# PE in the source's order through the attention, and score rows written bank by bank

## The chip, the cores and the metric

The kernel runs on one core of a Trainium2 chip. The metric is device microseconds of one execution. TensorE (PE) does the matmuls, VectorE (DVE), ScalarE (ACT) and GpSimd (POOL) the rest, and SyncE (SP) issues the DMAs. Each engine works through its own list of instructions in a fixed order and waits on semaphores for the others.

## The reference

Two layers of a block with three branches that read one normalised input: a Mamba-2 scan, grouped-query attention (four heads of 64) and differential attention (four heads, each with two softmax maps that share their values). The width is 1024, and there are 256 context tokens ahead of 1024 latent ones. This case is about the two attention branches:

```python
def block(qblk):
    s = jnp.einsum('bqgrd,bsgd->bgrqs', qblk, k).astype(jnp.float32) * scale
    p = jax.nn.softmax(s, axis=-1).astype(v.dtype)
    return jnp.einsum('bgrqs,bsgd->bqgrd', p, v)
...
o = attention(q[:, :, 0::2], k[:, :, 0::2], v) - lam * attention(q[:, :, 1::2], k[:, :, 1::2], v)
...
o_l = jnp.concatenate([y_s_l, y_g_l, y_d_l], axis=-1) @ w_out[l]
```

Context tokens read context alone, latent tokens read both (1280 keys). The second layer gives no context output.

## The kernel before

**Jobs.** Each layer has a projection and scan stage, then an attention stage, then a tail. The attention stage (from line 1226) works through jobs. A job is one head of one kind (0: grouped-query, keys in tile `gk`; 1: differential, keys in `dk`) for two or four tiles of 128 queries, and `CORD` orders the jobs of the last four query tiles: gk, dk, dk, gk, dk, dk, gk, gk. A job is taken in halves of two query tiles. A full half has five **steps**, one for each two of the ten key tiles; layer 0 has 168 steps and layer 1 has 160.

**Scores.** `s_rows` (line 1228) scores a pair of rows of 128 x 1280. A pair is two query tiles of a gk head, or the two maps of one query tile of a dk head. It takes five PSUM banks `sc` of a pool of three (`NSC`): two of 512 for the first row, one that holds the last 256 of both rows, two of 512 for the second. PE writes them (line 1239; two matmuls for a bank of 512 in a gk head, one in a dk head, so 12 and 6 for a pair), DVE copies each bank to `pt` and keeps its minimum (line 1241), reduces the minima (1252), and ACT takes the exponential with a row sum (1254). For a dk pair DVE then makes a factor `cc` (1284, 1285) and subtracts the second map from the first in 1024 columns (1289); POOL does the other 256 (1293, 1294).

**A step.** `w_front` transposes four 128 x 128 blocks of `pt` on PE (1369) into one of two PSUM tiles `tp`; ACT copies that to `pf` (1379), DVE or ACT rounds it to `ph` (1391, 1389), and POOL computes the remainder `pl` (the helper on line 128). `w_back` multiplies `ph` and `pl` with the values (1411, 1412) for the step two before (`LAG` is 3). After a job `out_b` folds the result (`pr`, 1335) and `y_out` transposes it (1309). Each step also takes its share of `fills`: the output projection (`ops`, lines 342 to 344) and, in layer 0, the modulation of the next layer (`mps`, line 149), whose weights `wm` come in pairs of 512 KB into the three buffers of tag `wo`.

**The source's order.** The loop at the end of `block_kernel` writes a step as `w_front`, then scores if any are owed, then `w_back`, then `out_b`/`y_out` that are due, then fills. Scores are owed when the share of the score work done is under the share of the value work done plus a lead of 30 (`LEAD`, in units of a quarter step), and while fewer than eight of the ten `pt` buffers are taken. Ahead of the first step of a half, every pair that the half needs and that isn't written yet is written at once. `s_next` (1449) writes a whole pair.

**The program's order.** The tile scheduler takes these instructions with priorities from the source's order (`w_front` and `w_back` are put 50 places ahead) and places them, engine by engine, by readiness in a timeline of its own. So PE's list isn't the source's: a score or a transpose can stand ahead of value matmuls that were written earlier.

**Loads.** When the last pair of a job is written, `prefetch` loads the next head of its kind: `dk` (1049, 1280 KB) and `q` (1050), or `q` alone or with `gk` (1043, 1042). `dk`, `gk` and each kind's `q` have one buffer, so these loads wait for the last score matmul that reads the old head.

Of the kernel before, what the change touches and what calls it, by code (L numbers as in the profile page):

```python
# [14 lines left out]
PSUM = bass.MemoryType.PSUM  # L15
# [28 lines left out]
CORD = ((0, 0), (1, 0), (1, 1), (0, 1), (1, 2), (1, 3), (0, 2), (0, 3))  # L44
TRIG = 12, 6
ILV = 0
SPC = 0
CSEQ = ((0, 0), (0, 1), (1, 0), (1, 1), (2, 0), (2, 1), (3, 0), (3, 1), (4, 0), (4, 1), (5, 0), (5, 1), (6, 0), (6, 1), (7, 0), (7, 1))
SCR = 1.3
MP = 1, 2  # L50
# [11 lines left out]
NSC, NTP, NPO, NXO = 3, 2, 1, 2  # L62
# [5 lines left out]
def block_kernel(ctx: ExitStack, tc: tile.TileContext, tok, cvec, wmod, pack,  # L68
# [4 lines left out]
    def pool(name, bufs=1, **kw):  # L73
        return tc.tile_pool(name=name, bufs=bufs, reuse_waits="tile", **kw)
# [354 lines left out]
    for l in range(DEPTH):  # L429
# [794 lines left out]
        wlast = [o7.tile([P, 8, P], F32R, name=f"wlast{i}") for i in range(2)]  # L1224

        with pool("att", 2) as ap, pool("attX", NXO, space=PSUM) as aX, pool("attO", NPO, space=PSUM) as aO, \
                pool("attS", NSC, space=PSUM) as aS, pool("attT", NTP, space=PSUM) as aT_:
            def s_rows(jb, pair):

                full = jb.nk == NT  # L1230
# [218 lines left out]
            def s_next():  # L1449
# [3 lines left out]
                with shifted(HPS):  # L1453
                    while s_at:
                        if next(s_at[0], 1):
                            s_at.pop()
                        if SPC:
                            break
# [163 lines left out]
```

## Time and profile before

| | us |
|---|---|
| time, median of 3 runs | 2074.26 (2069.14 to 2074.6) |
| the profiled execution | 2063.46 |
| its span, first to last instruction | 2061.6 |
| PE busy | 1806.6 (88%) |
| DVE busy | 1428.5 (69%) |
| POOL busy | 1211.7 (59%) |
| ACT busy | 1041.5 (51%) |

The profiled execution was 10.8 us shorter than the median. The attention stages are the stretches 604 to 1092 us and 1614 to 2025 us of the span. A busy PE in this profile is a union of overlapping matmuls with modelled ends, so a gap in it is surely idle, and a busy stretch need not be PE at its peak.

### The profile page before, as it was taken

To read this page: it belongs to the slowest core of one execution; us is meant where nothing else is said; L and a number is where in the kernel's file an instruction comes from. 1 tells how busy PE (TensorE), PEld (TensorE's weight loads), DVE (VectorE), ACT (ScalarE), POOL (GpSimd) and SP (SyncE) were. 2 spreads that over 40 slices of the span, in tenths; PEclk is the share of its full clock that TensorE was granted. 3 is DMA by queue.
4 is the path that set the end of the run, shared out by engine and by line. 5 is a ranking of instruction groups with operands and counts; after the bars stand their busy time and mean duration, and the time that the engine had idled before them with its cause. 6 is when DMAs were issued, how large, how long until landed. Compare 5 with 4: busy or idle time off the path is not lost. (4 is left out here: it accounts for less than half of the span.)

```text
span 2061.6 us, 30333 instructions
## 1 busy us (share of the span) xinstructions
PE 1806.6 (88%) x9936; PEld 1471.4 (71%) x9936; DVE 1428.5 (69%) x3286; ACT 1041.5 (51%) x1955; POOL 1211.7 (59%) x1135
## 2 busy tenths in 40 slices
PE   4899989899879999988988799888899899989895
PEld 3677777787668667876775487777777777878783
DVE  4777566766538776698866578468656588788954
ACT  3445233334437775766654345234244477777661
POOL 3626245747616676777755326466567378787761
PEclk9899999899999999998989899999999999999897
DMA  9157546776786788786656138667766866557545
GB/s 290 47 170 271 152 165 191 236 235 176 222 259 198 245 263 257 234 256 202 211 191 214 63 102 280 226 183 231 244 202 204 260 185 192 157 155 237 161 152 205
DMA packets 359998, 418.57 MB, mean 203 GB/s; under 512 B 38753, under 2 KB 252833, under 8 KB 359841
## 3 DMA queue, kind: packets, MB, share of 16 engines
q1 hardware_dynamic: 359840, 416.64, 65.1%
q8 instruction: 78, 1.28, 0.3%
q14 instruction: 80, 0.65, 0.1%
HBM read 282.18 MB, written 134.38 MB: 202 GB/s over the span
## 5 line engine op out<-in xcount | busy, mean ns | idle before, releaser
L128 POOL TENSOR_TENSOR pl<-pf,ph 128x512 fp32r<-128x512 f32 x283 | 373.6, 1325 | 189.0 <-DVE ph L1391 69.7
L1241 DVE TENSOR_SCALAR_CACHE_REDUCE pt<-sc 128x512 f32<-128x512 f32 (+1 forms) x600 | 334.2, 587 | 78.5 <-PE sc L1239 63.4
L958 PE MATMUL prj<-wh,u 128*128 128x512 f32 (+1 forms) x768 | 296.6, 389 | 33.0 <-DVE th L964 18.1
L1254 ACT ACTIVATE pt<-pt,nm 128x1280 f32<-128x1280 f32 x192 | 262.3, 1366 | 92.1 <-DVE nm L1252 91.0
L959 PE MATMUL prj<-wl,u 128*128 128x512 f32 (+1 forms) x768 | 294.8, 384 | 10.3 <-POOL wl L128 7.8
L960 PE MATMUL prj<-wh,u 128*128 128x512 f32 (+1 forms) x768 | 291.7, 380 | 0.0
L1369 PE MATMUL tp<-ident,pt 128*128 128x128 f32 x1312 | 209.3, 285 | 14.0 <-ACT pt L1254 5.6
L1379 ACT COPY pf<-tp 128x512 f32<-128x512 f32 x289 | 166.8, 581 | 74.9 <-PE tp L1369 49.3
L1412 PE MATMUL po<-pl,vt 128*128 128x256 f32 x644 | 183.1, 307 | 15.6 <-POOL pl L128 14.7
L958 PEld LDWEIGHTS prj<-wh,u 128*128 128x128 f32 x768 | 151.8, 199 | 62.5 <-DVE th L964 19.9
L1411 PE MATMUL po<-ph,vt 128*128 128x256 f32 x644 | 186.0, 303 | 5.2 <-DVE ph L1391 2.9
L1369 PEld LDWEIGHTS tp<-ident,pt 128*128 128x128 f32 x1312 | 162.1, 147 | 37.9 <-ACT pf L1379 10.7
L959 PEld LDWEIGHTS prj<-wl,u 128*128 128x128 f32 x768 | 152.0, 198 | 38.0 <-POOL wl L128 11.2
L960 PEld LDWEIGHTS prj<-wh,u 128*128 128x128 f32 x768 | 151.7, 198 | 23.5
L1239 PE MATMUL sc<-dk,q 128*128 128x512 f32 (+1 forms) x400 | 146.1, 408 | 15.2 <-DVE pt L1241 12.0
L1412 PEld LDWEIGHTS po<-pl,vt 128*128 128x128 f32 x644 | 126.3, 196 | 33.0 <-POOL pl L128 25.3
L1411 PEld LDWEIGHTS po<-ph,vt 128*128 128x128 f32 x644 | 127.2, 197 | 19.4 <-DVE ph L1391 5.6
L606 DVE SCALAR_TENSOR_TENSOR cacc<-craw,hw,cacc 128x1284 f32<-128x1284 f32 (+1 forms) x64 | 120.0, 1877 | 28.0 <-ACT cacc L603 12.0
L581 PE MATMUL prj<-u,wTh 128*128 128x512 f32 x256 | 109.8, 429 | 22.2 <-DVE u L209 14.2
L1239 PE MATMUL sc<-gk,q 128*128 128x256 f32 (+1 forms) x400 | 110.0, 385 | 19.9 <-DVE pt L1241 16.7
L342 PE MATMUL ops<-y,wo 128*128 128x512 f32 (+1 forms) x304 | 117.7, 387 | 10.5 <-DMA y<-y 6.3
L582 PE MATMUL prj<-u,wTh 128*128 128x512 f32 x256 | 109.3, 427 | 7.4 <-DVE u L128 6.8
(277 smaller groups left out, 4310.7 us busy)
## 6 DMA issues: line engine op xcount, KB each, us to landing
wo<-wo SPq DMA_DIRECT2D x80, 512.0 KB, 4.9
wm<-in_wmod_dram SPq DMA_DIRECT2D x48, 512.0 KB, 6.2
dk<-dk SPq DMA_DIRECT2D x16, 1280.0 KB, 7.9
ab<-acs SPq DMA_DIRECT2D x18, 1024.0 KB, 7.5
wo<-wos SPq DMA_DIRECT2D x32, 512.0 KB, 3.7
wf<-in_wtok_dram SPq DMA_DIRECT2D x64, 256.0 KB, 4.4
y<-y SPq DMA_DIRECT2D x30, 512.0 KB, 5.7
op<-o SPq DMA_DIRECT2D x48, 256.0 KB, 4.4
```

The lines of the kernel that those rows point to most:

```text
L128: eng.tensor_tensor(out_, full, hi.bitcast(F32), op=ALU.subtract)
L606: V.scalar_tensor_tensor(acc[:, a0:1284], raw[:, a0 + j:1284 + j], hw[:, i * 5 + j:i * 5 + j + 1], acc[:, a0:1284], op0=ALU.mult, op1=ALU.add)
L958: TE.matmul(ps[:, c0:], uh, wh[k][:, c0:], start=k == 0, stop=False)
L959: TE.matmul(ps[:, c0:], uh, wl[k][:, c0:], start=False, stop=False)
L960: TE.matmul(ps[:, c0:], ul, wh[k][:, c0:], start=False, stop=k == KT - 1)
L1239: TE.matmul(ps[:, 0:b - a].rearrange("p (t c) -> p t c", c=P), q[:, jb.q0 + j], kt[:, a // P:b // P], start=x == 0, stop=x == len(qq) - 1)
L1241: V.tensor_scalar(ts[r][:, a:b], ps[:, 0:b - a], -1.0, None, op0=ALU.mult, op1=ALU.min, accum_out=mts[r][:, i:i + 1])
L1254: S_.activation(e, e, AF.Exp, bias=nm, scale=-1.0, accum_out=jb.s2[:, j, mp_:mp_ + 1])
L1369: TE.transpose(tp[:, j * P:(j + 1) * P], jb.pt[2 * hf + j % 2][:, cs(2 * s + j // 2)], ident)
L1379: S_.copy(pf[:, :w_], tp[:, :w_])
L1411: TE.matmul(o, vv, a[:, c], start=k == 0, stop=False)
L1412: TE.matmul(o, vv, b[:, c], start=False, stop=k == jb.nk - 1)
```

## The change

`SPC` goes from 0 to 1: `s_next` leaves its loop after one piece of a pair, so an owed score is one bank (one of the five pieces; a sixth call does the dk combination). The rule by which scores are owed is the same, and it is asked again before each piece. And the attention stage runs under a manual schedule for PE: PE's instructions of this stage keep the order in which the source writes them. DVE, ACT, POOL and SP are still placed by the scheduler.

```diff
--- before.py
+++ after.py
@@ -44,7 +44,7 @@
 CORD = ((0, 0), (1, 0), (1, 1), (0, 1), (1, 2), (1, 3), (0, 2), (0, 3))
 TRIG = 12, 6
 ILV = 0
-SPC = 0
+SPC = 1
 CSEQ = ((0, 0), (0, 1), (1, 0), (1, 1), (2, 0), (2, 1), (3, 0), (3, 1), (4, 0), (4, 1), (5, 0), (5, 1), (6, 0), (6, 1), (7, 0), (7, 1))
 SCR = 1.3
 MP = 1, 2
@@ -1224,7 +1224,8 @@
         wlast = [o7.tile([P, 8, P], F32R, name=f"wlast{i}") for i in range(2)]
 
         with pool("att", 2) as ap, pool("attX", NXO, space=PSUM) as aX, pool("attO", NPO, space=PSUM) as aO, \
-                pool("attS", NSC, space=PSUM) as aS, pool("attT", NTP, space=PSUM) as aT_:
+                pool("attS", NSC, space=PSUM) as aS, pool("attT", NTP, space=PSUM) as aT_, \
+                tc.manual_schedule(engines={mybir.EngineType.PE}):
             def s_rows(jb, pair):
 
                 full = jb.nk == NT
```

Below, `tp` are the transposes of a step, `sc` the scores (from `dk` or `gk` keys), `po` the value matmuls, `ops` the projection, `mps` the modulation, `bps` a broadcast row. In the changed kernel lines past 1227 are one higher.

PE before, layer 1, while the scores of the last dk head's second half are written; other work stands between the banks:

```order
L1239 MATMUL sc<-dk,q 128x512
L1369 MATMUL tp<-ident,pt 128x128 x4
L1412 MATMUL po<-pl,vt 128x256
L1411 MATMUL po<-ph,vt 128x256
L1412 MATMUL po<-pl,vt 128x256
L1239 MATMUL sc<-dk,q 128x512
L1239 MATMUL sc<-dk,q 128x256
L1369 MATMUL tp<-ident,pt 128x128 x4
L1239 MATMUL sc<-gk,q 128x512 x2
L1409 MATMUL po<-pf,vt 128x256 x2
```

PE now, at the start of that head's second half:

```order
L194 MATMUL bps<-ident,nrr 128x128 x4
L1240 MATMUL sc<-dk,q 128x512 x2
L1240 MATMUL sc<-dk,q 128x256 x2
L1240 MATMUL sc<-dk,q 128x512 x4
L1240 MATMUL sc<-dk,q 128x256 x2
L1240 MATMUL sc<-dk,q 128x512 x2
L1370 MATMUL tp<-ident,pt 128x128 x4
L1412 MATMUL po<-ph,vt 128x256
L1413 MATMUL po<-pl,vt 128x256
```

All banks of both pairs of this half stand in one block, and the transposes that read these very rows come right behind it; nothing of another step is between.

PE before, layer 1, from the last rows ahead of the first score on a newly loaded dk head (`dk_19057`); the last score on the old one (`dk_18424`) stands 35 instructions above it:

```order
L1412 MATMUL po_16198<-pl_18771,vt_17999 128x256
L1411 MATMUL po_16198<-ph_18790,vt_17999 128x256
L1335 MATMUL pr_18851<-fold_78,ot_18674 128x64 x2
L1412 MATMUL po_16198<-pl_18791,vt_17999 128x256
L1411 MATMUL po_16198<-ph_18790,vt_17999 128x256
L1412 MATMUL po_16198<-pl_18791,vt_17999 128x256
L1369 MATMUL tp_18890<-ident_67,pt_18507 128x128
L1369 MATMUL tp_18890<-ident_67,pt_18508 128x128
L1369 MATMUL tp_18890<-ident_67,pt_18507 128x128
L1369 MATMUL tp_18890<-ident_67,pt_18508 128x128
L1411 MATMUL po_16198<-ph_18843,vt_17999 128x256
L1239 MATMUL sc_19137<-dk_19057,q_19056 128x512
```

PE now, the same change of heads (`dk_18509` to `dk_19135`):

```order
L1240 MATMUL sc_19106<-dk_18509,q_18508 128x512
L1412 MATMUL po_16205<-ph_19048,vt_18068 128x256
L1413 MATMUL po_16205<-pl_19049,vt_18068 128x256
L1412 MATMUL po_16205<-ph_19048,vt_18068 128x256
L1413 MATMUL po_16205<-pl_19049,vt_18068 128x256
L1370 MATMUL tp_19121<-ident_67,pt_18694 128x128
L1370 MATMUL tp_19121<-ident_67,pt_18801 128x128
L1370 MATMUL tp_19121<-ident_67,pt_18694 128x128
L1370 MATMUL tp_19121<-ident_67,pt_18801 128x128
L1240 MATMUL sc_19144<-dk_19135,q_19134 128x512
```

Between the last score on the old head and the first on the new one eight matmuls are left, one step's value matmuls and the next one's transposes. In layer 0 the same place has 21 in between (70 before).

PE before, layer 0, in the modulation of the next layer:

```order
L149 MATMUL mps<-wm,s_82 32x512 x2
L1239 MATMUL sc<-gk,q 128x512 x2
L1239 MATMUL sc<-gk,q 128x256 x2
L1239 MATMUL sc<-dk,q 128x256
L149 MATMUL mps<-wm,s_82 32x512 x2
L1411 MATMUL po<-ph,vt 128x256
L1335 MATMUL pr<-fold,ot 128x64 x2
L1239 MATMUL sc<-dk,q 128x256
L149 MATMUL mps<-wm,s_82 32x512 x2
L1412 MATMUL po<-pl,vt 128x256
```

PE now, there:

```order
L149 MATMUL mps<-wm,s_82 32x512 x4
L1370 MATMUL tp<-ident,pt 128x128 x4
L1240 MATMUL sc<-dk,q 128x512 x2
L1412 MATMUL po<-ph,vt 128x256
L1413 MATMUL po<-pl,vt 128x256
L1412 MATMUL po<-ph,vt 128x256
L1413 MATMUL po<-pl,vt 128x256
L149 MATMUL mps<-wm,s_82 32x512 x4
L1370 MATMUL tp<-ident,pt 128x128 x4
```

The two weights of one k stand together, once in a step, in 16 of 19 steps; before, they were taken one at a time, over some 34 steps.

The blocks like the first one, scores right ahead of the transposes that read them, stand in each layer where the late halves begin. In layer 0: 5 matmuls of a dk pair (twice), 8 of two dk pairs, 12 of two dk pairs, 2 and 12 and 12 of a gk pair. In layer 1: 4 of a dk pair (twice), 8 and 12 of two dk pairs, 12 and 12 of a gk pair. Layer 1 also begins with such a block of 12 (gk), with 18 more scores behind its transposes; in the order before all 18 of the first stand ahead of the transposes.

## Rows read from the trace of the kernel before

**Rows 1.** Window, us; busy us (count): PE, PEld, DVE, ACT, POOL; clock, DMA share, GB/s.

```profile
604.00:1092.00 488.00, 443.49 (x2706) 361.07 (x2704) 370.85 (x1089) 322.31 (x592) 328.08 (x325) 0.95 0.74 229
1614.00:2025.00 411.00, 365.72 (x2210) 311.41 (x2208) 321.57 (x940) 283.61 (x484) 286.97 (x259) 0.96 0.62 189
```

**Rows 2.** Waits of PE, attention of layer 0: us, times, longest us.

```profile
PE sc L1239 <- DVE pt L1241: 11.8, 19, 2.2
```

**Rows 3.** Waits of PE, attention of layer 1.

```profile
PE sc L1239 <- DVE pt L1241: 16.9, 24, 2.3
PE po L1412 <- POOL pl L128: 11.2, 14, 2.0
PE tp L1369 <- ACT pt L1254: 5.6, 1, 5.6
```

**Rows 4.** Groups by shape, attention of layer 1: busy us, mean ns, idle before.

```profile
L1369 PE MATMUL tp<-ident,pt 128*128 128x128 f32 x640 | 101.6, 285 | 7.0 <-ACT pt L1254 5.6 <-ACT pf L1379 1.2
...
L1289 DVE SCALAR_TENSOR_TENSOR pt<-pt,cc 128x1024 f32<-128x1024 f32 x32 | 52.4, 1639 | 0.5
...
L1285 DVE SCALAR_TENSOR_TENSOR cc<-s,nlam,cc 128x1 f32<-128x1 f32 x32 | 13.7, 427 | 0.4
...
L128 POOL TENSOR_TENSOR pl<-pf,ph 128x512 fp32r<-128x512 f32 x135 | 179.8, 1336 | 94.8 <-DVE nm L1252 30.7 <-DVE ph L1391 29.8 <-ACT ph L1389 16.1
L1293 POOL TENSOR_SCALAR pt<-pt,cc 128x256 f32<-128x256 f32 x32 | 35.3, 1103 | 12.7 <-DVE cc L1285 5.6 <-ACT pf L1379 3.6 <-ACT ph L1389 1.1
L1294 POOL TENSOR_TENSOR pt<-pt 128x256 f32<-128x256 f32 x32 | 29.6, 926 | 1.7
```

**Rows 5.** First gk pair of layer 1 in time: start us, us, what.

```profile
1614.20 4.62 PE L1239 MATMUL sc<-gk,q 128*128 128x512 f32 x18
1614.86 0.69 DVE L1241 TENSOR_SCALAR_CACHE_REDUCE pt<-sc 128x512 f32<-128x512 f32 x1 [4.59 <-PE sc L1239]
...
1615.47 0.69 DVE L1241 TENSOR_SCALAR_CACHE_REDUCE pt<-sc 128x512 f32<-128x512 f32 x1
...
1616.08 0.42 DVE L1241 TENSOR_SCALAR_CACHE_REDUCE pt<-sc 128x256 f32<-128x256 f32 x1
...
1616.43 0.69 DVE L1241 TENSOR_SCALAR_CACHE_REDUCE pt<-sc 128x512 f32<-128x512 f32 x1
...
1617.28 1.36 ACT L1254 ACTIVATE pt<-pt,nm 128x1280 f32<-128x1280 f32 x1 [7.73 <-DVE nm L1252]
...
1618.67 0.15 DVE L1252 TENSOR_REDUCE nm<-mt 128x1 f32<-128x3 f32 x1
```

**Rows 6.** The late stretches of layer 1 and layer 0, columns as in Rows 1.

```profile
1871.00:1992.00 121.00, 107.31 (x659) 92.35 (x659) 99.79 (x264) 85.12 (x147) 91.14 (x84) 0.94 0.53 169
904.00:1057.00 153.00, 127.76 (x717) 107.02 (x718) 132.13 (x354) 99.93 (x173) 111.85 (x102) 0.89 0.62 194
```

**Rows 7.** Loads dk (L1049) and q (L1050): SyncE ns min/median/max, landing us.

```profile
L1049 SPq DMA_DIRECT2D dk<-dk x7: 523/524/559, 642.7 to 955.7; - x7
...
DMA to landing us min/median/max: 7.0/7.3/9.3
...
L1050 SPq DMA_DIRECT2D q<-dq x15: 2352/3162/5681, 643.3 to 1902.6; - x15
...
DMA to landing us min/median/max: 7.7/9.2/11.2
```

**Rows 8.** The modulation: its matmuls on PE (L149), its loads (L159) and their landing.

```profile
L149 PE MATMUL mps<-wm,s x128: 592/605/617, 684.6 to 781.8; 128*32 128x512 f32 x128
L159 SPq DMA_DIRECT2D wm<-in_wmod_dram x32: 327/339/3269, 664.2 to 772.8; - x32
...
DMA to landing us min/median/max: 3.5/4.8/8.2
```

**Rows 9.** Two windows of 6 us at the start of layer 1, columns as in Rows 1.

```profile
1620.00:1626.00 6.00, 0.44 (x3) 0.20 (x2) 1.32 (x5) 1.94 (x3) 0.00 (x0) 0.73 1.07 354
1626.00:1632.00 6.00, 5.96 (x31) 5.36 (x31) 4.95 (x22) 5.02 (x8) 2.16 (x2) 0.70 0.97 333
```

## Prediction

> **What bounds the kernel now.** I read the two attention stretches as a whole first, since the change leaves the rest alone. PE is the busiest engine, 443.5 of 488 us and 365.7 of 411, with DVE next, 370.9 and 321.6, and ACT and POOL at about 70% [rows 1]. So a step in layer 1 takes 411 / 160 = 2.57 us, and DVE alone would need 321.6 / 160 = 2.01. PE's idle time is 44.5 and 45.3 us. It is in many short waits, no single one of which is the bound: for DVE to clear a score bank, 11.8 and 16.9 us [rows 2, 3], and in layer 1 for POOL's remainder `pl`, 11.2 [rows 3]. The longest one, 5.6 us, stands at the start of layer 1, where the first transposes wait for an exponential [rows 3]. These are what the change could remove; all of PE's idle time in both stages is 90 us, 4% of the execution. Where PE loses most is late in each stage, when score work is behind: 25.2 of 153 us in layer 0 and 13.7 of 121 in layer 1, and DVE is busier there than PE in layer 0 [rows 6].
>
> **What the change moves.** Nothing is added or removed; PE's 9936 instructions and all of the other engines' work stay. Three things in PE's list are new, and each is a place where the whole list now stands behind one wait. All sums are against the profiled execution, 2063.5 us.
>
> *A. Late halves, scores right ahead of their own transposes.* The rule for owing scores gives all pairs a common pace, but a dk job costs 6.4 units of score work and a gk job 2, for the same value work. The late query tiles come as gk, dk, dk, gk, dk, dk, gk, gk, so from the second dk job on the scores are behind, and the missing ones are written in one block when the half begins. In the order before, PE had other steps' work between them. Now the transposes behind the block wait for the whole chain, and value matmuls of older steps, projection and later scores stand behind these transposes. The first gk pair of layer 1 shows the chain [rows 5]: the first matmul starts at 1614.20, DVE takes the first bank at 1614.86, then needs 0.61 us for each bank of 512 and 0.35 for one of 256, and the second row's minimum is done at 1618.82; an exponential takes 1.36 us and reading its sum about 0.2, so both rows are ready at 1620.4, 6.2 us after the start. PE's own part is 12 of 18 matmuls that took 4.62 us, 3.1. So a gk block of 12 leaves PE idle for 3.1 us. A dk pair goes on with `cc`, 0.43 and a reciprocal, and the subtraction, 1.64 [rows 4]: after the last score 0.66 + up to three banks 1.9 + 0.15 + 1.55 + 0.6 + 1.64 + some hand-overs 0.2 = 6.7 us, of which 0.9 is PE's own, so 5.8 for a tail of four or five matmuls. A block of 8 has DVE busy with seven banks (4 x 0.61 + 2 x 0.61 + 2 x 0.35 = 4.4) and the first pair's `cc` and subtraction (2.3): 0.66 + 4.4 + 2.3 + 4.1 - 1.8 = 9.6. A block of 12 has ten banks (6.3): 13.3 - 2.6 = 10.7. A gk tail of two: 0.66 + 0.61 + 0.15 + 1.55 - 0.4 = 2.6. By the list of blocks: four gk blocks 12.4, four dk tails 23.2, two of eight 19.2, two of twelve 21.4, one gk tail 2.6, in all 79 us. The same stretches now hold 38.9 us of idle PE [rows 6], which I take to be replaced: **+40**. It could be +1, if the backlog that DVE, ACT and POOL clear meanwhile is given back at once, and +60 if the old waits stay beside the new ones.
>
> *B. A new dk head with no work ahead of it.* The load of `dk` and `q` starts when the old head's last score is done: 0.5 us for SyncE to issue the first, then 9.2 until `q` has landed [rows 7], say 10 us with the hand-over. In layer 1 only eight matmuls stand between, a step's transposes, 0.64 (101.6 us in 160 groups, [rows 4]), and four value matmuls, some 0.5 as an estimate; 8.9 us are open. In layer 0, with 21 between, some 7. Other changes of heads keep 88 matmuls or more between, or fall into a block of A. Less about 2 that PE waits there now: **+14**. Bounds: +4, if the engines behind catch up, and +18, by the longest landing, 11.2.
>
> *C. The modulation.* Its weights have three buffers. A load takes 0.34 us to issue, 4.8 to land, and its matmuls at least 0.6 [rows 8], so three loads go round in 5.7 us, one in 1.9, a pair in 3.8. Now a pair is due in each step of about 2.6 us. 16 pairs at 3.8 and three other steps at 2.57 make 68.5 us for 19 steps, which would otherwise take 48.8: 19.7. Before, the matmuls were spread from 684.6 to 781.8 [rows 8], some 34 steps, which at 2.57 would take 87.4: 10. **+10**, from 0 (the landings are median ones in a full queue, and SyncE may issue earlier) to +30 (landings of up to 8.2).
>
> *D. Starts.* In layer 1 eighteen scores stood ahead of the first transposes; now twelve, and the other eighteen pieces start after the wait. The wait itself is there already [rows 3]; DVE's 6 us for the second lot no longer lie beside it: +6, and some +2 in layer 0, where 30 scores stand alone. **+8**, from 0 to 12.
>
> *E. The even stream.* Elsewhere a bank is written every step or half step rather than in bursts, so PE should meet a free bank more often. Of 28.7 us of waits for banks [rows 2, 3] I let a quarter go: **-7**. This term is the least certain. PE can no longer pass a late `pl`: between a step's transposes and its value matmuls lie two steps, and each dk pair puts 1.10 + 0.93 us of POOL work ahead of some `pl` of 1.34 [rows 4]. I bound it by +40 and -64 (below).
>
> A to E: 40 + 14 + 10 + 8 - 7 = +65 us, 2128.5 for a profiled execution. That was 10.8 us under the median of the runs shown, so 2139 for a median; I say 2140.
>
> *The clock.* [...] I leave this out of the sum, since the steps behind the blocks are light (transposes and value matmuls alone, with POOL's 1.34 us a step as the floor), and take it into the upper end, 15 places, 27 us. [...]
>
> **Rivals.**
>
> *The even stream wins (faster).* Outside the late stretches lie 328 - 100 = 228 steps. A to D are 72 us, 0.32 a step: if these steps fall from 2.57 below 2.25 us the change is faster. DVE's floor is 2.01. Halfway to it, 2.29, the gain is 64 and nothing is won; at 2.15 it is 96, and the time 2074 + 72 - 96 = 2050. For it: DVE and PE are both under 90%, so the slack is in how they meet. Against it: outside the late stretches PE idles only 51 of 625 us [rows 1, 6], and it would have to find gain beyond that in what the profile calls busy. [...]
>
> *Every late remainder stops PE (slower still).* If the 64 dk pairs of both layers each hold PE for half of POOL's 2.0 us, and the bank waits stay, E is about +55 rather than -7: 2200.
>
> *It comes out even.* The blocks cost what the late stretches cost now (A at +1), and the rest cancels: 2070 to 2080. DVE is already the bound in layer 0's late stretch, 132 of 153 us [rows 6], which is what speaks for it.
>
> *The change doesn't do what it says.* PE's list shows the blocks and the steps as the source has them, so this has no chance worth a number.
>
> **How the numbers follow.** Slower as forecast, 2090 to 2180: 0.6. Slower still: 0.15. Even: 0.06. Faster: 0.19. About 0.3% (6 us) is what a measurement of this kernel can tell from no change, so faster 0.19, same 0.06, slower 0.75. The range leaves out the faster half of the faster cases and the top of the slowest: 2062 to 2205. The likeliest case's own range is 2090 to 2180.
>
> **What would show it.** In the changed kernel's trace, `tp` (line 1370) should wait for ACT and for the subtraction at about a dozen places, 3 to 11 us each, and these should lead PE's waits; `sc` should wait 7 to 9 us for `q` once in each layer; `mps` should wait for `wm` for about 10 us in all; waits of `sc` for DVE should fall below 28.7. The late stretches (the ten halves ahead of the last two) should grow from 153 and 121 us by 15 to 30 each. If the late stretches take no longer, A is wrong; if the other steps fall under 2.3 us, E is, and the change is faster.

## The result, and the profile after

The changed kernel takes 2328.6 us (median of 4 runs, 2313.4 to 2334.5) against 2071.7 (2065.1 to 2074.6): 1.1234 times, 95% interval 1.1168 to 1.13. Slower was right; 2140 and its range to 2205 were not. The loss of 257 us is about four times the 65 I had summed. Medians here and below leave out executions in a slower state of the chip, of which two of the kernels had one each.

The head of the page of after (span; then busy us, share and count of each engine) and PE's row and the clock in 40 slices:

```profile
span 2331.8 us, 30228 instructions
## 1 busy us (share of the span) xinstructions
PE 1874.3 (80%) x9936; PEld 1524.0 (65%) x9936; DVE 1413.6 (61%) x3286; ACT 1058.6 (45%) x1955; POOL 1212.8 (52%) x1137
...
PE   5898988899787788667588898988997878677576
...
PEclk8899999999898899888688899998997999888687
```

PE has as many instructions as before, yet is busy for 67.7 us more (1806.6 before). The rest is idle time. The two attention stages as a whole, then the early and the late part of each (columns as in [rows 1]):

```profile
603.00:1232.00 629.00, 477.96 (x2713) 389.25 (x2714) 357.93 (x1088) 332.92 (x594) 334.37 (x329) 0.86 0.59 180
1752.00:2295.00 543.00, 401.88 (x2215) 336.44 (x2213) 323.50 (x941) 291.62 (x484) 287.05 (x260) 0.85 0.49 148
...
603.00:973.00 370.00, 299.72 (x1791) 239.97 (x1792) 215.00 (x710) 214.88 (x396) 206.91 (x203) 0.91 0.66 201
973.00:1193.00 220.00, 144.77 (x739) 121.29 (x738) 128.16 (x348) 102.29 (x173) 113.94 (x103) 0.76 0.46 141
1752.00:2055.00 303.00, 233.52 (x1354) 197.11 (x1353) 199.04 (x599) 183.42 (x306) 178.85 (x162) 0.90 0.53 155
2055.00:2260.00 205.00, 137.42 (x685) 113.68 (x684) 110.34 (x311) 95.59 (x157) 99.08 (x91) 0.76 0.40 124
```

The late stretches took 153 and 121 us before [rows 6] and take 220 and 205: +67 and +84. The early stretches grew too, by some 70 and 46 us, and there I had expected a small gain. The window less PE's busy time gives PE's idle time: 151.0 and 141.1 us in the two stages, 292 in all, where they had 90 [rows 1]. These 202 us and the 68 us of busy time make up the 270 by which the profiled span grew. The late stretches hold 75.2 + 67.6 = 143 us of the idle time, 104 more than before [rows 6], so about half of the growth lies outside them. The clock fell to 0.76 in both late stretches (0.89 and 0.94 before, [rows 6]).

What PE waits for in layer 1 (us in total, times, longest), against [rows 3]:

```profile
PE sc L1240 <- DVE pt L1242: 52.5, 50, 2.9
PE tp L1370 <- DVE pt L1290: 27.3, 8, 6.7
PE yp L1310 <- POOL yk L1356: 21.6, 4, 6.6
PE tp L1370 <- ACT pt L1255: 18.0, 8, 8.8
PE sc L1240 <- DMA q<-dq: 8.0, 1, 8.0
PE po L1413 <- POOL pl L128: 5.5, 10, 1.0
PE tp L1370 <- DVE ri L1324: 3.9, 1, 3.9
```

The first line leads: waits of scores for a bank that DVE has to clear. In layer 1 they were 16.9 us and are 52.5; in layer 0, 11.8 [rows 2] and 65.5. Of these 118 us, 40 lie in the late stretches. Looked at in time, nearly all of them have one shape (layer 1, one gk pair; PE, its scores' DVE readers and the next PE work):

```profile
1813.50 0.94 PE L1240 MATMUL sc<-gk,q 128*128 128x512 f32 x4
...
1814.25 0.69 DVE L1242 TENSOR_SCALAR_CACHE_REDUCE pt<-sc 128x512 f32<-128x512 f32 x1 [0.83 <-PE sc L1240]
...
1814.87 0.42 DVE L1242 TENSOR_SCALAR_CACHE_REDUCE pt<-sc 128x256 f32<-128x256 f32 x1
1815.21 0.08 DVE L1242 DVE_READ_ACCUMULATOR pt<-sc 128x1 f32 x1
...
1815.35 0.51 PE L1240 MATMUL sc<-gk,q 128*128 128x256 f32 x2 [0.91 <-DVE pt L1242]
```

The four matmuls of the first line are two for a bank of 512 and two for the first row's last 256 columns (the trace prints the first one's shape). The two of the last line are the second row's last 256, which go into the other half of the same PSUM bank. They stand right behind, and start when DVE has read the first half: 0.91 us of PE idle, with value matmuls that nothing holds up queued behind. The two layers hold 96 pairs of full rows and 12 of context rows, which also share a bank. Over the whole program 108 of the 112 waits, with 115.0 of 118.6 us, are waits of a second half that stands right behind its first.

No run here let PE write the second half during that read, so whether it could isn't shown; what is shown is the wait as this program has it.

### The profile page after: what moved, and what is told of

Its sections match the earlier page's. It is cut to its first block, busy times and chain, and to the rows that moved or that the text cites. A ratio compares the mean times of both kernels' runs of the same rounds, so it can differ in the third digit from the quotient of the medians.

```text
span 2331.8 us, 30228 instructions
## 1 busy us (share of the span) xinstructions
PE 1874.3 (80%) x9936; PEld 1524.0 (65%) x9936; DVE 1413.6 (61%) x3286; ACT 1058.6 (45%) x1955; POOL 1212.8 (52%) x1137
## 5 line engine op out<-in xcount | busy, mean ns | idle before, releaser
L1242 DVE TENSOR_SCALAR_CACHE_REDUCE pt<-sc 128x512 f32<-128x512 f32 (+1 forms) x600 | 343.6, 591 | 256.0 <-PE sc L1240 253.8
L1370 PE MATMUL tp<-ident,pt 128*128 128x128 f32 x1312 | 234.2, 305 | 89.1 <-DVE pt L1290 47.6
L1370 PEld LDWEIGHTS tp<-ident,pt 128*128 128x128 f32 x1312 | 180.9, 158 | 149.2 <-issue 69.2
L1240 PE MATMUL sc<-dk,q 128*128 128x512 f32 (+1 forms) x400 | 169.2, 470 | 97.2 <-DVE pt L1242 83.4
L1240 PEld LDWEIGHTS sc<-dk,q 128*128 128x128 f32 x400 | 78.7, 218 | 120.9 <-DVE pt L1242 106.1
L1413 PEld LDWEIGHTS po<-pl,vt 128*128 128x128 f32 x644 | 136.2, 211 | 22.9 <-POOL pl L128 13.3
L1412 PEld LDWEIGHTS po<-ph,vt 128*128 128x128 f32 x644 | 137.2, 213 | 15.5 <-ACT ot L1417 9.1
L1240 PE MATMUL sc<-gk,q 128*128 128x512 f32 (+1 forms) x400 | 115.8, 411 | 36.0 <-DVE pt L1242 35.2
L581 PE MATMUL prj<-u,wTh 128*128 128x512 f32 x256 | 109.6, 428 | 21.2 <-DVE u L209 13.9
L342 PE MATMUL ops<-y,wo 128*128 128x512 f32 (+1 forms) x304 | 123.7, 407 | 0.1
```

The costliest lines, as they stand in the source:

```text
L342: TE.matmul(o, wa[:, k], y[:, :, 0], start=first, stop=False)
L1240: TE.matmul(ps[:, 0:b - a].rearrange("p (t c) -> p t c", c=P), q[:, jb.q0 + j], kt[:, a // P:b // P], start=x == 0, stop=x == len(qq) - 1)
L1242: V.tensor_scalar(ts[r][:, a:b], ps[:, 0:b - a], -1.0, None, op0=ALU.mult, op1=ALU.min, accum_out=mts[r][:, i:i + 1])
L1370: TE.transpose(tp[:, j * P:(j + 1) * P], jb.pt[2 * hf + j % 2][:, cs(2 * s + j // 2)], ident)
L1412: TE.matmul(o, vv, a[:, c], start=k == 0, stop=False)
L1413: TE.matmul(o, vv, b[:, c], start=False, stop=k == jb.nk - 1)
```

## The experiments

Theory S, formed from these rows: in a held order PE meets DVE inside a pair, since the third bank of a pair is written in two halves by one piece. The first rival, P: writing by the bank does the damage. The second, B: three banks are too few for a held order, whatever is in them. Ratios stand against the kernel before, run beside each (medians 2065.7 to 2071.7 us), and are the fairer comparison between rows. "bank" is PE's wait for DVE to clear a score bank and "tp" its transposes' wait for DVE's subtraction and ACT's exponential, in us over the whole program.

| kernel | us | ratio (95%) | PE busy | bank | tp |
|---|---|---|---|---|---|
| changed | 2328.6 | 1.1234 (1.1168 to 1.13) | 1874.3 | 118.6 | 80.1 |
| held order only | 2378.4 | 1.1511 (1.1472 to 1.155) | 1865.8 | 155.6 | 59.9 |
| by the bank only | 2083.5 | 1.008 (1.0045 to 1.0114) | 1811.4 | 30.1 | 9.5 |
| changed + own bank | 2259.5 | 1.0931 (1.0896 to 1.0966) | 1845.7 | 28.3 | 71.2 |
| changed + split | 2294.3 | 1.1097 (1.1055 to 1.1138) | 1854.7 | 79.5 | 89.6 |
| changed + filler | 2314.5 | 1.1202 (1.1172 to 1.1232) | 1908.7 | 61.6 | 75.9 |
| own bank + half ahead | 2247.6 | 1.0843 (1.0797 to 1.0889) | 1840.2 | 10.3 | 83.2 |
| own bank + three steps ahead | 2205.3 | 1.0677 (1.0631 to 1.0724) | 1836.9 | 4.7 | 13.3 |
| ... + yp and modulation moved | 2163.8 | 1.0471 (1.0427 to 1.0516) | 1817.3 | 8.0 | 14.1 |
| ... + values a step later | 2139.1 | 1.035 (1.0312 to 1.0388) | 1799.8 | 13.6 | 14.4 |
| the same source, scheduler's order | 2074.3 | 1.0029 (1.0011 to 1.0047) | 1811.1 | 10.8 | 7.1 |

**The two halves of the change, apart.**

```diff
-SPC = 1
+SPC = 0
```

> The held order alone: PE keeps the source's order, and the source emits both rows of a pair in one go, as the kernel before does. Theory S (a wait that nothing stands behind: in the held order PE meets DVE inside a pair of score rows) expects it to be worse still, since all six writes of a pair now stand in a row and only three banks take them: some 1.5 us of PE waiting for each of about 100 pairs, 2330 to 2450 us, and PE's waits of sc for DVE well over the 118 us of the changed kernel. Theory P (writing by the bank is what does the damage, and a held order is harmless) expects about 2070 to 2100.

```diff
-                pool("attS", NSC, space=PSUM) as aS, pool("attT", NTP, space=PSUM) as aT_, \
-                tc.manual_schedule(engines={mybir.EngineType.PE}):
+                pool("attS", NSC, space=PSUM) as aS, pool("attT", NTP, space=PSUM) as aT_:
```

> The bank at a time alone: the scheduler goes on choosing PE's order, and the source emits the score rows by the bank. Theory S expects the scheduler to fill each wait for DVE with other work, as before: 2050 to 2110 us, waits of sc for DVE below 45 us. Theory P expects most of the loss, 2250 or more.

Measured: 2378.4 and 2083.5. P falls. The held order alone costs 313 us, more than the change as a whole. Its bank waits are 155.6 us, and the wait of `po` for POOL's remainder, on which the prediction had put a bound but no sum, comes next:

```profile
PE po L1413 <- POOL pl L128: 49.2, 30, 2.9
```

Writing by the bank gives 50 us of that back, and under the scheduler it costs 0.8%.

**The shared bank.** Row 1's last 256 columns in a bank of their own:

```diff
-                both = bank()
...
-                    piece(r, 2 if full else 0, both[:, r * 256:r * 256 + 256], w_ - 256, w_)
+                    piece(r, 2 if full else 0, bank(), w_ - 256, w_)
```

> The changed kernel, but the last 256 columns of the second row go into a bank of their own rather than into the other half of the first row's (six banks a pair rather than five, still three buffers). Theory S: PE waits for DVE because the second half of the shared bank is written right behind the first, which DVE must have read; with its own bank the waits of sc for DVE fall from 118 us to 30 to 50, and the time from 2329 to 2230 to 2270 us. Rival B (three banks are too few for the held order, whatever is in them): more banks for each pair, so the waits stay at 110 us or rise, and the time is 2320 to 2360.

The same bank, but with the source broken off between its halves:

```diff
                     if r == 0:
                         ends.append(rest(0))
+                        yield
```

> The changed kernel, but the source breaks off between the two halves of the shared bank, so that a step's other work stands between them on PE (same banks, same buffers; a pair is six parts rather than five). Theory S: the second half finds the first one read; waits of sc for DVE fall from 118 us to 30 to 50, the time to 2230 to 2280 us. Rival B: as many banks in as many buffers, so no change, 2320 to 2340, with waits of over 100 us.

Measured: 2259.5 and 2294.3. With own banks a pair needs more of the three buffers, and still the bank waits fall to what they were before; B falls. PE's waits, own bank:

```profile
PE tp L1369 <- DVE pt L1289: 46.1, 15, 5.2
PE po L1412 <- POOL pl L128: 45.1, 48, 2.1
...
PE yp L1309 <- POOL yk L1355: 36.2, 9, 6.2
PE sc L1240 <- DVE pt L1242: 28.3, 42, 3.0
```

90 us of waits are gone, and 69 us of time (63 by the ratios). Part has a new name: `po` for `pl`, 7.9 us in the changed kernel, is 45.1; I take it that PE now comes to it earlier. The split went the way S said, but only by 34 us and to 79.5 us of bank waits, outside what I had expected of it. Two pieces often fall into one step, and then nothing stands between the halves: in 64 places of its trace the second half still waits right behind the first, and these hold 73.2 of the 79.5 us.

**Is it idle time, and what of the clock?** Eight harmless matmuls (zero weights, added into the open value sum) go ahead of row 1's half, at 76 places:

```diff
+                    if r == 1 and b - a == 256 and full and 0 <= at_s[0] <= 3:
+                        for _ in range(8):
+                            TE.matmul(po2[:, half[0] % 2, 0:P], zeror, identr, start=False, stop=False)
```

> The changed kernel with eight matmuls more (128 columns, zero weights, added into the open value sum) right ahead of row 1's half of the shared bank, at 76 of the places where PE waits there. Theory W (the wait ends when DVE has read row 0's half, whatever PE does meanwhile): these 608 matmuls lie in idle time, the waits for banks fall by about what they take, and the time does not rise, 2318 to 2336. Theory K (a good part of what was lost is clock, which fell since PE stood idle there): the clock rises from 0.887 and PE's other matmuls take less, 2290 to 2315. If PE was not truly waiting there (its recorded idle time is a modelled end), the matmuls add their own time, some 40 us: 2350 to 2380.

Measured: 2314.5; the interval overlaps that of the changed kernel, so the gain of 14 us (7 by the ratios) is not certain and W and K can't be told apart by the time, but a loss of 40 is ruled out. The profiled span is 2308.0 against 2331.8. The page of this run, then the busy time of the added matmuls alone by layer (window, us; PE busy, PEld busy; clock, DMA share, GB/s), then one of the places:

```profile
PE 1908.7 (83%) x10544; PEld 1571.4 (68%) x10544; DVE 1411.0 (61%) x3287; ACT 1055.8 (46%) x1955; POOL 1220.4 (53%) x1137
```

```profile
590.00:1240.00 650.00, 39.76 (x304) 38.86 (x304) 0.88 0.59 184
1735.00:2290.00 555.00, 40.50 (x304) 39.83 (x304) 0.90 0.49 152
```

```profile
1801.45 1.00 PE L1243 MATMUL po<-identr,zeror 128*128 128x128 f32 x8
...
1802.03 0.42 DVE L1247 TENSOR_SCALAR_CACHE_REDUCE pt<-sc 128x256 f32<-128x256 f32 x1
...
1802.52 0.50 PE L1245 MATMUL sc<-gk,q 128*128 128x256 f32 x2
```

A full microsecond of added work fits into this wait, and row 1's half starts as soon after DVE's read as in the changed kernel (0.07 us after its end, 0.06 there). In all, 80.3 us of added work took 57 us off the bank waits, so most of it lies in idle time. PE's other matmuls, taken by themselves, are busy for 1846.5 us, 28 less than the 1874.3 of the changed kernel, with the granted clock at 0.907 instead of 0.887.

The size of this gain is uncertain, since executions differ. The profiled one of the changed kernel has the lowest clock of its four (0.887 to 0.898). The run below that moves the modulation alone and leaves these waits as they are (113.7 us) has PE busy for 1856.1 us, 18 less, at 0.897. What holds in every execution is the direction: with the filler the clock is 0.901 to 0.908. So with waits of about a microsecond, one for each pair, the clock was lower than with 76 of them filled. How many of the 68 us are theirs isn't shown.

**The late blocks.** The scores of a half are owed evenly over the steps of the half before it:

```diff
-                            sdone[1] < stotal * (wdone + LEAD) / wtotal:
+                            sdone[1] < max(stotal * (wdone + LEAD) / wtotal, due(pos, s)):
...
+                return upto[pos] + (upto[pos + 1] - upto[pos]) * (s + 1) / steps[pos]
```

> The changed kernel, but the scores of a half are owed evenly over the steps of the half before it, so that no block of scores stands right ahead of its own transposes. Theory A (these blocks cost what the waits of tp for DVE and ACT show, 89 us in both layers, and some of the clock): waits of tp for DVE and ACT fall below 25 us, the late stretches from 220 and 205 us to 160 to 185 each, the time from 2329 to 2220 to 2265 us. Rival C (the late stretches are long because DVE and POOL are behind there, so that the waits come back under another name): tp waits fall, waits for banks and for pl rise as much, 2300 us or more.

> Both: a bank of its own for the second row's last 256 columns, and the scores a half ahead. If the shared bank and the blocks are separate causes, their gains add (70 us and some 80): 2160 to 2190 us. If they overlap (the waits inside the blocks were in part waits for the shared bank), 2190 to 2230. The granted clock should be back from 0.887 to 0.91 or more.

Measured: 2307.7 (1.1149, 1.1102 to 1.1195) without own banks and 2247.6 with them, 21 and 12 us under the same kernels without this edit. The first lies where rival C had put it and not in theory A's range, the second above both of its ranges. A block is gone, but its last bank still stands one step ahead of the transposes, and the `tp` waits stay (83.2 us). If the chain from the last score to the transposes is what costs, and not the block, more lead should help. So the same edit, three steps ahead:

```diff
             def due(pos, s):
+                s += 3
+                while pos < len(steps) and s >= steps[pos]:
+                    s -= steps[pos]
+                    pos += 1
```

> As the run with own banks and the scores a half ahead, but the scores of a half are done three steps before its first transposes, rather than in the step right before them. Theory A' (what the late halves pay is the chain from the last score over DVE's minimum, ACT's exponential and DVE's subtraction to the first transpose; scores that end in the step before still have it open): waits of tp for DVE and ACT fall from 83 us to below 25, the late stretches from 205 and 176 us to 165 and 145 or less, the time from 2248 to 2165 to 2195 us. Rival C (DVE and POOL are behind in the late stretches): within 20 us of 2248.

Measured: 2205.3, 42 us less. That is 10 us short of the range that I had expected, and the late stretches, 178 and 154 us, are above the 165 and 145. But the mechanism shows: they took 211 and 190 with own banks alone, `tp` waits are 13.3 us, and rival C falls. What leads now is POOL, and with the modulation's loads those of the dk heads, which, I take it, have fewer waits behind which to land. The windows of the late stretches, then PE's waits, with own banks and three steps ahead:

```profile
955.00:1133.00 178.00, 132.59 (x739) 116.70 (x738) 127.38 (x336) 98.46 (x170) 109.71 (x101) 0.81 0.58 173
1978.00:2132.00 154.00, 118.95 (x685) 102.08 (x684) 109.45 (x298) 91.26 (x155) 97.21 (x88) 0.87 0.52 159
```

```profile
PE po L1412 <- POOL pl L128: 53.1, 55, 2.3
PE mps L149 <- DMA wm<-in_wmod_dram: 41.2, 17, 14.8
PE sc L1240 <- DMA q<-dq: 37.2, 4, 11.5
PE yp L1309 <- POOL yk L1355: 33.8, 8, 6.2
```

**Output transposes and modulation.** `yp` a step later and the modulation over twice as many steps, first behind own banks and half ahead, then behind three steps ahead; and the modulation alone in the changed kernel:

```diff
-            yield 0.9
+            yield 1.8
...
-                    later.append((step_no[0] + 2, lambda: y_out(jb, blk, yk)))
+                    later.append((step_no[0] + 3, lambda: y_out(jb, blk, yk)))
```

> As the one before, and the transposes of the outputs (yp) stand a step later in the source and the modulation's blocks are spread over twice as many steps. Waits of yp for POOL were 31.6 us and of mps in the attention 14.6; if the held place of these two is what makes them wait, they fall below 15 and 5, and the time is 20 to 35 us under the run before it. If POOL is simply late, the waits only move: within 10 us.

> The run before, with the output transposes a step later and the modulation spread over twice as many steps. If these two causes are separate from the lead, their 64 us add: 2100 to 2135 us, the clock at 0.93 or more and PE's idle time in the two attention stretches near 130 us. If what they gave was only cover for the late chain: 2150 to 2190.

> The changed kernel with the modulation spread over twice as many steps, and nothing else. If the modulation costs what its waits show (14.6 us of mps for wm in the attention), 2312 to 2322 us. If waits there also lower the clock and let the engines behind run dry, more: 2285 to 2305. If it is the place of the output transposes that gave the 64 us above, 2320 or more.

Measured: 2183.1 (1.0554, 1.0528 to 1.0581), 64 us less where I had expected 20 to 35; 2163.8, 42 us less; and 2314.6 (1.1196, 1.1156 to 1.1236) for the modulation alone. The last one is 14 us less (8 by the ratios) with overlapping intervals, and agrees with the waits (`mps` in the attention 14.6 to 3.2 us). So some 28 to 50 us are left for `yp`, if the gains add; `yp` was not moved by itself, and its waits for POOL fell by 21 (37.9 to 17.1) and 14 us (33.8 to 19.4). That these edits are worth 64 us while the late chain is open and 42 once three steps cover it is the second of the two cases that I had put down for the run: part of what they gave was cover for that chain.

**POOL's remainder, and what is left.** The value matmuls one step further behind (ten buffers `pw` instead of eight), and then this same source with the scheduler's order:

```diff
-PWB = 8
+PWB = 10
-QB, PFB, PHB, LAG, PTB = 1, 2, 3, 3, 10
+QB, PFB, PHB, LAG, PTB = 1, 2, 3, 4, 10
```

> As the run with own banks, lead, output transposes and modulation moved, and the value matmuls one step further behind their transposes, with ten instead of eight buffers between. If po waits for POOL's remainder since it stands too close behind it in the held order (37 us of po for pl in the run with the scores a half ahead), these waits fall below 15 and the time by 15 to 35 us, to about 2090. If POOL is simply the slower engine there, the waits come back elsewhere, within 10 us.

> The source of the last run (own bank, by the bank, lead of three steps, output transposes and modulation moved, value matmuls a step further behind), but with the scheduler's order on PE instead of the held one. That run stood at 2139, 69 us over the kernel before. If these 69 us are what the held order itself still costs (PE's 35 us of waits for the dk heads, its waits for POOL, and the clock), the scheduler gives 2040 to 2075 us. If it is the source as it is now written that costs them, 2090 to 2140.

Measured: 2139.1, 25 us less (`po` for `pl` 41.8 to 11.9), and 2074.3. The same source, instruction for instruction, is 65 us faster when the scheduler sets PE's order. So what the edits leave comes with the held order. The other engines' lists differ with it, since the scheduler places them around PE's, and no run takes these apart. PE's waits there, with the order held:

```profile
PE sc L1240 <- DMA q<-dq: 33.2, 4, 10.6
PE mps L149 <- DMA wm<-in_wmod_dram: 33.1, 10, 14.8
PE yp L1309 <- POOL yk L1355: 19.7, 6, 5.3
```

**Do the repairs help the kernel before?** Own bank, and three steps ahead, each alone in it:

> The kernel before (the scheduler's order, a pair in one go), with a bank of its own for the second row's last 256 columns. If the scheduler hides the shared bank's wait by other work, nothing is gained: 2055 to 2085 us, against 2066 to 2072. If the shared bank costs there too, its waits of sc for DVE, 28.7 us, fall by half and the time by 10 us or more.

> The kernel before with the scores of a half done three steps ahead, nothing else. In the held order the lead was worth 42 to 54 us. If the scheduler already covers the late chain by passing it, the time is unchanged, 2060 to 2080. If the chain costs there as well (PE's idle time in the late stretches, 25 and 14 us), 2035 to 2058, and a version faster than both.

Measured: 2076.7 (1.0033, 1.0014 to 1.0053) and 2074.3 (1.0028, 1.0008 to 1.0047). No gain, rather 0.3% lost. The bank waits fall a little (28.7 to 22.5 and 25.0 us), and nothing comes of it. No version that I ran beats the kernel before.

## Why the prediction was wrong

**E, the even stream, is the step that failed.** It said that a bank is written every step or half step rather than in bursts, and let the bank waits fall by a quarter: -7 us. They rose by 90 us, to 118.6, of which 115.0 are the second half's; giving row 1 its own bank took them back to 28.3 and 69 us off the time. Outside the late stretches PE's idle time grew by 98 us, where E and its neighbours B, C and D had 25. I counted pieces, and took each for one write of one bank. One piece in five writes a bank twice, with DVE's read in between, which is a burst of two whose second write waits for that read (0.91 us in the pair above). It was to be read before the run: the diff's rule and the code of the third bank say it, and PE's new order shows that bank's two matmuls as one row of x2.

**The clock, left out of the sum, goes with 68 us of busy time; my upper end held 27 for it.** The same 9936 matmuls took that much longer. The clock records of both traces have two levels, 1.0 and 0.5 of full speed. In the trace of the changed kernel a transpose takes 0.27 us at the higher and 0.42 at the lower (medians), and 1314 matmuls ran at the lower level, where before it were 653. I looked only at the long waits, 15 of them, and reasoned that light steps behind them would not feel the clock. The 27 us took 1.8 us for each, 30% of the 6 us at 0.70 behind one wait [rows 9]; no run shows that loss for each of the 15 places, and what the runs showed in its place is the 68 us. With 76 of the many short waits filled the clock was 0.907 in the profiled execution instead of 0.887; what they cost stays open. In both late stretches the clock was 0.76, and no run here separates that from the waits that it goes with.

**A, the late halves, had the blocks about right and a wrong subtraction.** I took 79 us of idle time in the blocks and let the old 39 be replaced. In the trace the thirteen blocks, with the transposes behind them, hold some 92 us. But the late stretches hold 143: the other 51 stand beside the blocks, among them 17 us of `yp` and four waits for the subtraction, 3.0 to 3.5 us each, with no block ahead. So the step that failed in A is "which I take to be replaced"; the stretches grew by 67 and 84 us and not by 15 to 30, and the `tp` waits, 80.1 us, did not lead PE's waits. The blocks themselves scatter. One of 12, for which I had 10.7 us, in layer 0 (1.19 + 1.05 + 1.70 + 3.61 = 7.6 us idle), then the costliest, at the second half of the last dk job of layer 1, PE, then DVE:

```profile
1114.95 3.00 PE L1240 MATMUL sc<-dk,q 128*128 128x256 f32 x6 [1.19 <-DVE pt L1242]
1118.99 1.43 PE L1240 MATMUL sc<-dk,q 128*128 128x256 f32 x3 [1.05 <-DVE pt L1242]
1122.13 0.45 PE L1370 MATMUL tp<-ident,pt 128*128 128x128 f32 x1 [1.70 <-DVE pt L1290]
1126.19 0.87 PE L1370 MATMUL tp<-ident,pt 128*128 128x128 f32 x3 [3.61 <-DVE pt L1290]
```

```profile
2187.71 0.86 PE L1240 MATMUL sc<-dk,q 128*128 128x256 f32 x3 [1.40 <-DVE pt L1242]
2191.13 1.40 PE L1240 MATMUL sc<-dk,q 128*128 128x512 f32 x2 [2.56 <-DVE pt L1242]
2192.95 0.58 PE L1240 MATMUL sc<-dk,q 128*128 128x256 f32 x1 [0.42 <-DVE pt L1242]
2196.39 1.44 PE L1240 MATMUL sc<-dk,q 128*128 128x256 f32 x3 [2.86 <-DVE pt L1242]
2204.51 0.45 PE L1370 MATMUL tp<-ident,pt 128*128 128x128 f32 x1 [6.68 <-DVE pt L1290]
2209.32 0.87 PE L1370 MATMUL tp<-ident,pt 128*128 128x128 f32 x3 [4.36 <-DVE pt L1290]
```

```profile
2200.21 0.75 DVE L1208 SCALAR_TENSOR_TENSOR ol<-ol,mG,rb 128x512 f32<-128x512 f32 x1 [2.00 <-DMA ol<-o]
2200.88 0.68 DVE L1242 TENSOR_SCALAR_CACHE_REDUCE pt<-sc 128x512 f32<-128x512 f32 x1
...
2201.71 0.66 DVE L1210 TENSOR_TENSOR ol<-ol 128x512 f32<-128x512 f32 x1
2202.29 0.74 DVE L1208 SCALAR_TENSOR_TENSOR ol<-ol,mG,rb 128x512 f32<-128x512 f32 x1
2202.95 0.14 DVE L1253 TENSOR_REDUCE nm<-mt 128x1 f32<-128x3 f32 x1
2203.02 1.35 DVE L1290 SCALAR_TENSOR_TENSOR pt<-pt,cc 128x1024 f32<-128x1024 f32 x1
```

The second one has 1.40 + 2.56 + 0.42 + 2.86 + 6.68 + 4.36 = 18.3 us. I had DVE free for the block. Its list, which the scheduler still orders, puts the output's scaling (`ol`) between the banks and the subtraction, and the first of these waits 2.0 us for a load. Three steps of lead gave back 54 us over own banks alone; that this lies between the +40 and the +60 that I had for A is luck, since the late stretches are still longer than before (178 and 154 us against 153 and 121).

**B and C were near.** `sc` waits for `q` once in each layer, 5.7 and 8.0 us (7 and 8.9 predicted). `mps` waits 14.6 us in the attention (1.8 before), and spreading it gave some 14, with overlapping intervals, for a term of +10. **D** was not tested by itself; the first wait of layer 1 for an exponential is 8.8 us, against 5.6 [rows 3], and the first half's idle time is 7 us longer.

**A term was missing:** `yp` behind POOL's product `yk`. In both layers together it waited 0.4 us before and 31.6 after, and the move of `yp` was worth some 28 us or more, if the gains add. In *C* and *B* I had asked of each instruction what stands ahead of it now, and I did not ask it of this one.

**The rivals.** *Every late remainder stops PE* was nearest in time, 2200, and its mechanism was there, but not in the changed kernel: there `po` waits for `pl` under 9 us, and 45 once the bank waits are gone. That bank waits give POOL the time is not the whole of it, since the held order alone has 49.2 us of this wait beside 155.6 of bank waits. *The even stream wins* fell with E.

## What to carry to other kernels

When an order is held, take each instruction on that engine and ask what it waits for and what in the list stands between the two; count writes of a bank and reads that must come between them, not pieces of source. A PSUM bank that is filled in two goes, with a read of the first half between them, had 115.0 us of waits here under the held order; a second bank took 69 us off the time, and other work between the goes, where it stood there, 34. A scheduler that passes a wait hides faults of the source, so the same repair may be worth 69 us under a held order and nothing under the scheduler.

## What the runs showed of the hardware

I had not expected the clock to differ with waits of about 1 us, one in each pair, at all. With 608 useless matmuls in 76 of them the granted clock was 0.901 to 0.908 in six executions, and 0.887 to 0.898 in the four of the changed kernel. In the profiled pair (0.907 and 0.887) PE's own matmuls took 28 us less and the span was 24 us shorter, but the medians differ by 14, within their intervals, and another kernel that keeps these waits had 18 of those 28 us as well.
